# Weight matmuls of a load kept together on TensorE in the input projection's blocks and the values' product

## The chip, the core and the metric

The kernel runs on one core of a Trainium2 chip. The core has a matrix engine (TensorE, PE in the profile, with its weight loads listed as PEld), a vector engine (VectorE, DVE), a scalar engine (ScalarE, ACT), GpSimd (POOL) and SyncE (SP), which here issues the DMAs. Each engine works through its own stream of instructions in order, and semaphores hold an instruction until what it needs is done. The metric is the device time of one execution in microseconds (us). Lower is better.

## What is computed

The reference is a decoder trunk of two layers on one sequence of 256 tokens with 2048 channels. Each layer has a token mixer with two head groups (RWKV-7 time mixing, and sparse attention with three branches) that read one common input projection, then an output projection, a normalization, a squared-ReLU MLP and a second normalization. A conditioning vector gives shifts, scales and gates. Cut to its frame:

```python
for i in range(DEPTH):
    mod = cond @ w_ada[i] + b_ada[i]
    sh_m, sc_m, gt_m, sh_f, sc_f, gt_f = [m[:, None, :] for m in jnp.split(mod, 6, axis=-1)]
    h = x * (1 + sc_m) + sh_m
    u = h @ w_in[i]
    o_rwkv, v_first = _rwkv7_mix(u[..., :RWKV_COLS], v_first, ...)
    o_nsa = _nsa_mix(u[..., RWKV_COLS:], cmp_pos, cmp_w1, cmp_w2)
    y = jnp.concatenate([o_rwkv, o_nsa], axis=-1) @ w_out[i]
    x = _layer_norm(DN_ALPHA * x + (1 + gt_m) * y, ln1_g[i], ln1_b[i])
    h = x * (1 + sc_f) + sh_f
    y = jnp.square(jax.nn.relu(h @ mlp_w1[i])) @ mlp_w2[i]
    x = _layer_norm(DN_ALPHA * x + (1 + gt_f) * y, ln2_g[i], ln2_b[i])
```

All weights are float32 and each is read from memory once.

## The kernel before

**Channels on partitions.** An activation is 16 tiles of 128 channels by 256 tokens. A float32 product is made of three matmuls of a faster 32-bit form: weight and activation are each split into a rounded high part and the rest, and high by high, rest by high and high by rest are added up (`mm3`, L235). The modulated input of a layer is kept as 16 such pairs in the list `hs`: `hhi` and `hlo` in the profile.

**A load.** `unit` (L218) fetches 512 KB of weights into `wf` (5 buffers) by one DMA and splits them in two halves of 512 columns. For each half ScalarE casts `wh` (L226) and VectorE subtracts to get `wl` (L227). `wh` and `wl` have four buffers each, so two loads' worth. `part` gives the slices of 128 (or more) columns.

**A block.** `block` (L243) makes 128 output channels from 16 products: two loads `u` of eight products `k` each, so 2 x 24 weight matmuls of 128x128 by 128x256 into one accumulator bank of PSUM. Two banks exist for it (`acc`). Then `evict` takes the result out; `fill` lets a conditioning step come between loads in layer 0. `block` is called for the input projection `win` with `hs`, for the output projection `wout` with the pairs of `mix`, and for the MLP's `w1` and `w2`. Other forms of the same products are `kouter` (several outputs side by side) and `start` (the first columns of layer 0, under an order written by hand); the change leaves them alone.

**The values' product.** The columns of two of the value projections are computed the other way round, tokens on partitions (L814 to L824): eight loads `q`, each with two channel tiles `k`, two token halves `i` and three matmuls of 128x128 by 128x512, into two accumulators `va`, which share the banks of `acc`.

**What stands beside them.** A layer's mixer has, in the order of the text: the r and k columns and `rwkv_a` for four head pairs of the first half (`half_in`); `rwkv_b`, a triangular inverse, mostly on VectorE; `rwkv_c`, a recurrence over four chunks, in which products of 64 columns (`up`, `zp`, `sp`, `op`) alternate with copies on ScalarE and VectorE; `rwkv_out`; four blocks and four more for the compressed, selected and window keys, with `rope` on their results; `compress`; the second half of the recurrence; the values' product; and for each of eight pairs of heads a query block with `rope` and `attend`, a chain of scores (`cs`, `sc`), softmax, transposes (`ct`, `pt`) and outputs (`ot`). In layer 0 groups of eight conditioning products (`gv`, L206, from `ada_pe`) come in between. All these products are small float32 matmuls, mostly of another stationary operand each.

**What sets the order.** A planner orders each engine's stream: among the instructions that are ready by its own estimate of times it takes the one of highest priority, which is the order of the text unless raised by `high_priority`. So a block's weight matmuls, later in the text, go wherever a small product earlier in the text isn't ready yet, one matmul at a time. `issue_after(x)` puts what follows on x's engine behind x. Together, `with tc.issue_after(first), tc.high_priority(3000000)` make a group that follows its first instruction closely; the scores and outputs in `attend` and the conditioning products are grouped in that way already. The chip then runs the stream as planned, whatever the real durations are.

In the 60 blocks of `win` that run through `block` (24 in layer 0, 36 in layer 1) and in the values' product, every weight matmul stands by itself for the planner.

Of the kernel before, what the change touches and what calls it, by code (L numbers as in the profile page):

```python
# [167 lines left out]
def tile_trunk(tc, ap, outT, dbg=None):  # L168
    nc = tc.nc
    V, A, G, PE, SY = nc.vector, nc.scalar, nc.gpsimd, nc.tensor, nc.sync  # L170
    with ExitStack() as ctx:
# [6 lines left out]
        def st(tag, shape, dt=FT, name=None):  # L178
            if dbg is not None:
                dbg.setdefault("_sz", {})  # L180
                dbg["_sz"][tag] = max(dbg["_sz"].get(tag, 0), int(np.prod(shape[1:])) * 4 * BUFS.get(tag, 1))
            return sb.tile(shape, dt, name=name or tag, tag=tag, bufs=BUFS.get(tag, 1))
# [7 lines left out]
        def accb(shape, name="acc", tag="acc"):  # L190
            return psp.tile(shape, FT, name=name, tag=tag, bufs=2)
# [13 lines left out]
        def mm(o, l, r, start=True, stop=True):  # L205
            return PE.matmul(o, l, r, start=start, stop=stop, skip_group_check=True)  # L206
# [11 lines left out]
        def unit(src):  # L218
            wf = st("wf", [128, 1024])
            SY.dma_start(wf, src)  # L220
            out = []
            for i in range(2):
                wh, wl = st("wh", [128, 512], FR), st("wl", [128, 512], FR)
                s = slice(i * 512, i * 512 + 512)
                with tc.high_priority(1000000):
                    A.copy(wh, wf[:, s])  # L226
                    V.tensor_sub(wl, wf[:, s], wh.bitcast(FT))  # L227
                out.append((wh, wl))

            def part(o, n=128):  # L230
                s = slice(o % 512, o % 512 + n)
                return out[o // 512][0][:, s], out[o // 512][1][:, s]
            return part

        def mm3(o, w, x, first, last):  # L235
            (wh, wl), (xh, xl) = w, x
            mm(o, wh, xh, first, False)
            mm(o, wl, xh, False, False)
            mm(o, wh, xl, False, last)
# [3 lines left out]
        def block(src, u0, xs, evict, rot=False, prio=500000):  # L243
            bank = accb([128, 2, T])
            acc = bank[:, 0]
            for u in range(2):
                w = unit(src[u0 + u])
                for k in range(8):
                    mm3(acc, w(k * 128), xs[u * 8 + k], u + k == 0, u * 8 + k == 15)
                if fill[0]:  # L250
                    fill[0](1)
                count[0] += 1
            with tc.high_priority(prio):
                evict(acc, bank[:, 1]) if rot else evict(acc)
# [103 lines left out]
        hs = []  # L358
# [51 lines left out]
        for l in range(NL):  # L410
# [7 lines left out]
            win = ap["win"][l]  # L418
# [20 lines left out]
            if l == 0:  # L439
                with tc.manual_schedule(engines={PE.engine}):  # L440
                    for _ in first(0):
                        pass
                    sums = [st("TM", [128, 2, T], name="sum") for _ in range(6)]
                    pair = st("SV", [128, 2, 2, T], name="sum")
                    sums += [pair[:, 0], pair[:, 1]] + [st("TM", [128, 2, T], name="sum") for _ in range(2)]
                    start(win, hs, first, sums)
                for b in range(16):
                    ev0(b, sums[b // 2][:, b % 2])
            else:
                kouter(win, 0, hs, ev0)  # L450
                for b in range(8, 12):
                    block(win, 16 + 2 * (b - 8), hs, lambda acc, b=b: ev0(b, acc))
# [227 lines left out]
            def half_in(half):  # L680
                H = {"UR": [[None] * 2 for _ in range(4)], "TM": [[None] * 2 for _ in range(4)], "BK": [[None] * 2 for _ in range(4)],
                     "bv": [None] * 4, "SV": [st("SV", [128, 4, 4, 64], name="SV") for _ in range(2)],
                     "PC": st("PC", [128, 4, 4])}
                for p in range(4):
                    pi = half * 4 + p
                    for i in range(2):
                        b = 12 + 2 * pi + i
                        if l > 0 or b >= NS:
                            block(win, 2 * b if half == 0 else 2 * (b + 8), hs, lambda acc: ev0(b, acc))
                        elif b >= 16:  # L690
                            ev0(b, sums[b // 2][:, b % 2])
                    rwkv_a(pi, p, rkt.pop(2 * pi), rkt.pop(2 * pi + 1), H)
                return H
# [41 lines left out]
            u = 40  # L735
            cin = [[None] * 2 for _ in range(2)]
            for kv in range(2):
                for gp in range(2):
                    t = slab(name="cin")
                    cin[kv][gp] = t  # L740
                    block(win, u, hs, lambda acc, rp, t=t: rope(acc, rp, t) if kv == 0 else A.copy(t, acc), True)
                    u += 2
# [70 lines left out]
            u = 72  # L813
            va = [accb([128, 512], "va") for _ in range(2)]  # L814
            for q in range(8):
                w = unit(win[u + q])
                for k in range(2):
                    xh, xl = hs[2 * q + k]
                    wh, wl = w(k * 512, 512)
                    for i in range(2):  # L820
                        c = slice(i * 128, i * 128 + 128)
                        mm(va[i], xh[:, c], wh, q + k == 0, False)
                        mm(va[i], xl[:, c], wh, False, False)
                        mm(va[i], xh[:, c], wl, False, q + k == 8)  # L824
            u += 8
            Vt = []
            for i in range(2):
# [77 lines left out]
            for j in range(8):  # L905
                q = st("rk" if j < 4 else "S", [128, T], name="q")
# [165 lines left out]
            hs = []  # L1072
# [11 lines left out]
            y = [st("TM", [128, 2, T], name="y") for _ in range(8)]  # L1084
# [43 lines left out]
            if l == 0:  # L1128
                hs = []
# [25 lines left out]
```

## Time and profile before

| what | value |
|---|---|
| median of the runs | 2805.02 us (3 runs, 2801.45 to 2806.73) |
| the profiled execution | 2805.57 us, span of its core 2803.7 us |
| granted TensorE clock, mean | 0.981 |
| weight casts on ScalarE and subtractions on VectorE | 1536 each |
| input projection by `block`, layer 0 | 24 blocks, 48 loads, 1152 weight matmuls |
| input projection by `block`, layer 1 | 36 blocks, 72 loads, 1728 weight matmuls |
| values' product, per layer | 8 loads, 96 weight matmuls |

The profile comes from one execution. Its page has the busy time of each engine, the chain of work that ended last, and the costliest groups of instructions; a line such as L206 is the line of a helper (`mm`), so the tile names tell which product is meant. The timeline lists instructions by start time and merges equal neighbours. Ends of matmuls are modelled and overlap, so the distance from one start to the next is the better measure of pace. The busy time by stretch has a row for each stretch, with each engine's busy time, the granted clock and the DMA share.

### The profile page before, as it was taken

To read this page: it belongs to the slowest core of one execution; us is meant where nothing else is said; L and a number is where in the kernel's file an instruction comes from. 1 tells how busy PE (TensorE), PEld (TensorE's weight loads), DVE (VectorE), ACT (ScalarE), POOL (GpSimd) and SP (SyncE) were. 2 spreads that over 40 slices of the span, in tenths; PEclk is the share of its full clock that TensorE was granted. 3 is DMA by queue.
4 is the path that set the end of the run, shared out by engine and by line. 5 is a ranking of instruction groups with operands and counts; after the bars stand their busy time and mean duration, and the time that the engine had idled before them with its cause. 6 is when DMAs were issued, how large, how long until landed. Compare 5 with 4: busy or idle time off the path is not lost.

```text
span 2803.7 us, 59395 instructions
## 1 busy us (share of the span) xinstructions
PE 2682.2 (96%) x22794; PEld 2450.1 (87%) x22794; DVE 2088.5 (74%) x4710; ACT 1507.1 (54%) x3221; POOL 69.6 (2%) x205
## 2 busy tenths in 40 slices
PE   6999899998999999999999999999999999999997
PEld 4777678756999999999999888887799999999997
DVE  3677868656789788888998786886796566666567
ACT  3344345554585554645557544556567565464555
POOL 0000010000000000000000001000000000000000
PEclk9999999898999999999999999999999999999998
DMA  8986656386579899999986444333466777776664
GB/s 302 320 271 229 239 190 196 121 265 211 171 231 370 316 344 339 338 352 336 342 266 200 140 150 129 120 107 119 157 197 187 235 217 235 231 233 205 195 191 126
DMA packets 206780, 639.63 MB, mean 228 GB/s; under 512 B 23392, under 2 KB 42848, under 8 KB 206496
## 3 DMA queue, kind: packets, MB, share of 16 engines
q1 hardware_dynamic: 206496, 635.83, 68.0%
q8 instruction: 179, 2.93, 0.4%
q14 instruction: 105, 0.86, 0.1%
HBM read 629.45 MB, written 6.29 MB: 227 GB/s over the span
## 4 chain that ended last, share of the span: by engine, by line
PE 78%; DVE 13%; DMA 4%; ACT 3%; issue 2%; SPq 0%; ACTq 0%; POOL 0%; DVEq 0%
PE acc L206 65%; DVE wl L227 4%; PE gv L206 2%; DMA wap<-in_wad 1%; ACT wh L226 1%; PE ot L206 1%; PE pt L896 1%; PE mt L206 1%; DMA wf<-in_win 1%; DVE Tt L577 1%; DVE fs L575 1%; PE va L206 1%; PE vp L206 1%; PE tp L206 0%; PE rb L206 0%
## 5 line engine op out<-in xcount | busy, mean ns | idle before, releaser
L226 ACT CAST wh<-wf 128x512 fp32r<-128x512 f32 x1536 | 946.1, 620 | 859.0 <-PE acc L206 483.4
L227 DVE TENSOR_TENSOR wl<-wf,wh 128x512 fp32r<-128x512 f32 x1536 | 1038.5, 689 | 384.2 <-ACT wh L226 372.8
L206 PE MATMUL acc<-hhi,wh 128*128 128x256 f32 x3456 | 983.5, 285 | 17.1 <-ACT wh L226 8.8
L206 PE MATMUL acc<-hhi,wl 128*128 128x256 f32 x3456 | 972.3, 281 | 8.7 <-DVE wl L227 8.5
L206 PE MATMUL acc<-hlo,wh 128*128 128x256 f32 x3456 | 971.9, 282 | 0.2 <-DVE hlo L407 0.2
L206 PE MATMUL acc<-hi,wh 128*128 128x256 f32 x2560 | 714.8, 279 | 8.1 <-DVE res L1059 3.8
L206 PE MATMUL acc<-lo,wh 128*128 128x256 f32 x2560 | 715.4, 280 | 1.3 <-DVE lo L215 1.3
L206 PE MATMUL acc<-hi,wl 128*128 128x256 f32 x2560 | 714.8, 279 | 0.1
L206 PEld LDWEIGHTS acc<-hhi,wh 128*128 128x128 f32 x3456 | 656.8, 190 | 61.2 <-issue 24.1
L206 PEld LDWEIGHTS acc<-hhi,wl 128*128 128x128 f32 x3456 | 655.7, 190 | 18.2 <-DVE wl L227 12.9
L206 PEld LDWEIGHTS acc<-hlo,wh 128*128 128x128 f32 x3456 | 654.6, 190 | 8.7 <-issue 4.5
L206 PEld LDWEIGHTS acc<-hi,wh 128*128 128x128 f32 x2560 | 484.6, 189 | 10.5 <-ACT hi L214 5.0
L206 PEld LDWEIGHTS acc<-lo,wh 128*128 128x128 f32 x2560 | 483.3, 189 | 3.6 <-DVE lo L215 2.4
L206 PEld LDWEIGHTS acc<-hi,wl 128*128 128x128 f32 x2560 | 484.1, 189 | 1.4 <-issue 0.8
L344 DVE CUSTOM_DVE_ANT_0 wa<-wa,cond,modh 128x1024 f32<-128x1024 f32 x112 | 143.3, 1279 | 0.0
L344 DVE CUSTOM_DVE_ANT_0 wa<-wa,cond,vec 128x1024 f32<-128x1024 f32 x112 | 143.3, 1279 | 0.0
L206 PE MATMUL gv<-wap,cT 128*32 128x512 f32 x640 | 90.6, 639 | 21.7 <-DMA wap<-in_wad 21.4
L1099 DVE TENSOR_TENSOR lo<-relu,hi 128x256 fp32r<-128x256 f32 x128 | 54.1, 425 | 45.5 <-ACT relu L1098 45.3
L288 DVE TENSOR_TENSOR sum<-sum,acc 128x512 f32<-128x512 f32 x70 | 48.1, 687 | 45.8 <-PE acc L206 45.8
L883 ACT ACTIVATE P<-P,tyn 128x128 f32<-128x128 f32 (+1 forms) x128 | 57.3, 448 | 11.8 <-DVE tyn L881 11.1
L1097 ACT ACTIVATE hi<-relu 128x256 fp32r<-128x256 f32 x128 | 53.5, 422 | 3.5
L1098 ACT ACTIVATE relu<-relu 128x256 f32<-128x256 f32 x128 | 53.3, 420 | 3.6
(290 smaller groups left out, 2352.5 us busy)
## 6 DMA issues: line engine op xcount, KB each, us to landing
wf<-in_w SPq DMA_DIRECT2D x512, 512.0 KB, 4.6
wa<-in_wada SPq DMA_DIRECT2D x224, 512.0 KB, 5.6
wf<-in_win SPq DMA_DIRECT2D x192, 512.0 KB, 4.1
wap<-in_wad SPq DMA_DIRECT2D x208, 256.0 KB, 4.7
wf<-in_wout SPq DMA_DIRECT2D x64, 512.0 KB, 4.1
wap<-in_wad SPq DMA_DIRECT2D x56, 512.0 KB, 5.1
cw<-in_cw SPq DMA_DIRECT2D x16, 512.0 KB, 4.1
xin<-in_xT SPq DMA_DIRECT2D x16, 128.0 KB, 5.5
```

The costliest lines, as they stand in the source:

```text
L206: return PE.matmul(o, l, r, start=start, stop=stop, skip_group_check=True)
L226: A.copy(wh, wf[:, s])
L227: V.tensor_sub(wl, wf[:, s], wh.bitcast(FT))
L288: V.tensor_add(s, s, bank)
L344: V.tensor_tensor_reduce(wa, wa, cb, 0.5, init, OP.mult, OP.add, dst)
L575: V.tensor_mul(x, Mu[:, j + 1:32, j:j + 1].to_broadcast([128, n, w]), Tt[:, j:j + 1, 0:w].to_broadcast([128, n, w]))
L577: V.tensor_sub(Tt[:, j + 1:32, 0:w], Tt[:, j + 1:32, 0:w], x)
L883: A.activation(P[:, h, c:c + n], P[:, h, c:c + n], AF.Exp, bias=m[:, 2 * h + i:2 * h + i + 1], scale=-1.0, accum_out=z[:, 2 * h + i:2 * h ...
L896: PE.transpose(pt[:, h, c * 128:c * 128 + 128], P[:, h, 256 * i + c * 128:256 * i + c * 128 + 128], ident)
L1097: A.activation(hi, t, AF.Square)
L1098: A.activation(t, t, AF.Square)
L1099: gate[0] = V.tensor_sub(lo, t, hi.bitcast(FT)).ins
```

## The change

In `block`, when the source is the input projection and the activations are `hs`, the 24 weight matmuls of a load are issued in another order and as a group. The products go from `k` = 7 down to 0, and in each from `wl` by `hhi` over `wh` by `hhi` to `wh` by `hlo`, so that the first matmul reads the second half's `wl`, which is the last operand to be made. The other 23 follow it directly at raised priority. The accumulator's start flag moves to the new first matmul of the first load and the stop flag to the last of the second. All other calls of `block` keep the old order.

In the values' product the 12 matmuls of a load are grouped in the same way: channel tile 1 before 0, the products with `wl` first, both token halves in turn.

```diff
--- before.py
+++ after.py
@@ -245,8 +245,16 @@
             acc = bank[:, 0]
             for u in range(2):
                 w = unit(src[u0 + u])
-                for k in range(8):
-                    mm3(acc, w(k * 128), xs[u * 8 + k], u + k == 0, u * 8 + k == 15)
+                if xs is not hs or src is not win:
+                    for k in range(8):
+                        mm3(acc, w(k * 128), xs[u * 8 + k], u + k == 0, u * 8 + k == 15)
+                else:
+
+                    trio = lambda k: [(w(k * 128)[i], xs[u * 8 + k][j]) for i, j in ((1, 0), (0, 0), (0, 1))]
+                    ops = [o for k in range(7, -1, -1) for o in trio(k)]
+                    with tc.issue_after(mm(acc, *ops[0], u == 0, False).ins), tc.high_priority(3000000):
+                        for i, o in enumerate(ops[1:]):
+                            mm(acc, *o, False, u == 1 and i == 22)
                 if fill[0]:
                     fill[0](1)
                 count[0] += 1
@@ -814,14 +822,16 @@
             va = [accb([128, 512], "va") for _ in range(2)]
             for q in range(8):
                 w = unit(win[u + q])
-                for k in range(2):
+                ops = []
+                for k in range(1, -1, -1):
                     xh, xl = hs[2 * q + k]
                     wh, wl = w(k * 512, 512)
-                    for i in range(2):
-                        c = slice(i * 128, i * 128 + 128)
-                        mm(va[i], xh[:, c], wh, q + k == 0, False)
-                        mm(va[i], xl[:, c], wh, False, False)
-                        mm(va[i], xh[:, c], wl, False, q + k == 8)
+                    for x, y in ((xh, wl), (xh, wh), (xl, wh)):
+                        ops += [(i, x[:, i * 128:i * 128 + 128], y) for i in range(2)]
+                run = lambda n: mm(va[ops[n][0]], *ops[n][1:], q == 0 and n < 2, q == 7 and n >= 10)
+                with tc.issue_after(run(0).ins), tc.high_priority(3000000):
+                    for n in range(1, 12):
+                        run(n)
             u += 8
             Vt = []
             for i in range(2):
```

## The prediction

> **What bounds the kernel now.** First the page: how long the span is, which engine is full, what the chain that ended last is made of.
>
> ```profile
> span 2803.7 us, 59395 instructions
> ...
> PE 2682.2 (96%) x22794; PEld 2450.1 (87%) x22794; DVE 2088.5 (74%) x4710; ACT 1507.1 (54%) x3221; POOL 69.6 (2%) x205
> ...
> PE 78%; DVE 13%; DMA 4%; ACT 3%; issue 2%; SPq 0%; ACTq 0%; POOL 0%; DVEq 0%
> ```
>
> TensorE bounds the kernel on average. The change touches only the stretches that hold the projection's blocks, so the next view is the busy time by stretch: two of layer 0, two of layer 1, and one of the MLP to compare with.
>
> ```profile
> core 0: us, PE busy (x) PEld busy (x) DVE busy (x) ACT busy (x) POOL busy (x), PEclk, DMA share, GB/s
> 2200.00:2300.00 100.00, 100.00 (x879) 100.00 (x878) 56.67 (x87) 55.50 (x105) 0.00 (x0) 1.00 0.67 208
> ...
> 200.00:475.00 275.00, 259.51 (x2109) 202.93 (x2108) 209.21 (x583) 127.99 (x322) 23.43 (x75) 0.95 0.65 218
> 475.00:665.00 190.00, 174.94 (x1510) 120.65 (x1510) 114.36 (x452) 103.92 (x316) 5.62 (x12) 0.92 0.56 186
> 1520.00:1830.00 310.00, 297.85 (x2445) 260.13 (x2445) 243.60 (x637) 158.67 (x371) 20.53 (x71) 0.99 0.44 136
> 1830.00:2006.00 176.00, 164.01 (x1527) 130.54 (x1525) 125.31 (x463) 108.72 (x321) 5.56 (x10) 0.98 0.34 108
> ```
>
> In the MLP 879 matmuls start in 100 us: one per 0.114 us, the pace of a weight matmul in an unbroken row. The four stretches are 951 us long and hold 897 us of busy TensorE. They are nearly full too, but there the weight matmuls are mixed with the small float32 products of the recurrence and of the attention. The timeline of TensorE shows what the mixing costs (start, duration, instruction):
>
> ```profile
> 1723.05 0.69 PE L206 MATMUL zp<-Us,TM 128*64 128x64 f32 x16
> 1723.66 0.38 PE L206 MATMUL acc<-hlo,wh 128*128 128x256 f32 x1
> 1723.89 0.28 PE L206 MATMUL acc<-hhi,wh 128*128 128x256 f32 x1
> 1724.00 0.29 PE L206 MATMUL acc<-hhi,wl 128*128 128x256 f32 x1
> 1724.12 0.28 PE L206 MATMUL acc<-hlo,wh 128*128 128x256 f32 x1
> 1724.38 0.30 PE L206 MATMUL sp<-ZV,BK 128*64 128x64 f32 x2
> 1724.61 0.39 PE L206 MATMUL acc<-hhi,wh 128*128 128x256 f32 x1
> ```
>
> Four weight matmuls stand between two small products. From the first's start to the next small product's start is 1724.38 - 1723.66 = 0.72 us, where four at the unbroken pace are 0.46. The second starts 0.23 after the first instead of 0.11, and the small product 0.26 after the last instead of 0.11. I call such a stretch of weight matmuls a **run**. Over all runs of the four stretches I took the time from a run's first start to the next other start, less 0.114 per matmul: the median is 0.21 us, whatever the run's length. That is the price of going in and out of a run once.
>
> Then I counted. The projection's block matmuls stand in 131 runs in layer 0 (first and last start below) and 131 in layer 1.
>
> ```profile
> 204.36 0.47 PE L206 MATMUL acc<-hhi,wh 128*128 128x256 f32 x1
> ...
> 599.26 0.39 PE L206 MATMUL acc<-hhi,wh 128*128 128x256 f32 x1
> ...
> 1522.30 0.47 PE L206 MATMUL acc<-hhi,wh 128*128 128x256 f32 x1
> ...
> 1925.48 0.37 PE L206 MATMUL acc<-hlo,wh 128*128 128x256 f32 x1
> ```
>
> The 24 blocks of layer 0 and 36 of layer 1 are 120 loads of 24 matmuls. Numbering the matmuls shows 222 breaks inside a load, in 78 of the 120 loads, and 40 between loads; 176 of the runs are seven matmuls or shorter.
>
> **The change, part by part.** No matmul, cast or load is added or taken away, and no DMA is moved past a queue. Two things change: the order of TensorE's stream, and the moment from which a load may start.
>
> Switches removed. After the change a load's 24 matmuls are one run, so there are at most 120 runs where 262 were: 142 fewer at 0.21 us, **-30 us**. This is the careful end: where loads follow each other without a break, as many do already, there are fewer runs still. If all 222 inner breaks went and none came between loads, it would be 222 x 0.21 = 47 us.
>
> The small products' side. A group of them that is torn by a run costs more as well:
>
> ```profile
> 1727.98 0.30 PE L206 MATMUL up<-SV,UR 128*64 128x64 f32 x2 [0.42 <-DVE SV L640]
> 1728.21 0.39 PE L206 MATMUL acc<-hlo,wh 128*128 128x256 f32 x1
> ...
> 1728.65 0.68 PE L206 MATMUL up<-SV,UR 128*64 128x64 f32 x14
> 1729.26 0.39 PE L206 MATMUL acc<-hhi,wl 128*128 128x256 f32 x1
> ```
>
> Here 16 products take 0.23 + 0.61 = 0.84 us in two pieces; the 16 of zp above take 0.61 in one. Most groups are not torn but wait for another engine between them, so I take nothing and keep 142 x 0.23 = 33 us as the far end.
>
> At this switch a rule of the Trainium skill speaks against the change. TensorE: Matmul & The Clock Gate, "Part 2: What happens when you issue a matmul", says that TensorE pulls weight loads ahead of matmuls in flight, so that the next tile's weights load while the last one's matmul runs. By it a switch would cost nothing and the 30 us above would be zero. The weight loads of the same run disagree:
>
> ```profile
> 1723.66 0.19 PEld L206 LDWEIGHTS acc<-hlo,wh 128*128 128x128 f32 x1
> 1723.77 0.19 PEld L206 LDWEIGHTS acc<-hhi,wh 128*128 128x128 f32 x1
> ```
>
> The second load starts 0.12 before its matmul (1723.89); the first starts with its matmul, not before it. In this trace the pull-ahead stops at the switch.
>
> The values' product. Its 16 loads of 12 matmuls stand in 21 runs now, of which the first six-matmul run is this:
>
> ```profile
> 441.78 0.59 PE L206 MATMUL va<-wh,hhi 128*128 128x512 f32 x1
> ...
> 443.36 0.50 PE L206 MATMUL tp<-cst,a 128*128 128x2 f32 x4
> ```
>
> Six take 1.58 us, 0.20 more than six at its usual 0.23. At least five runs go: **-1 us**.
>
> Pauses that lose their cover. The short runs are what the planner slips in while a small product waits for VectorE or ScalarE. One such stretch, the recurrence over four chunks of the first half in layer 1, by groups, and its busy time:
>
> ```profile
> L206 PE MATMUL acc<-hlo,wh 128*128 128x256 f32 x20 | 6.3, 317 | 0.0
> L206 PE MATMUL acc<-hhi,wh 128*128 128x256 f32 x20 | 6.1, 306 | 0.0
> L206 PE MATMUL acc<-hhi,wl 128*128 128x256 f32 x20 | 6.0, 301 | 0.0
> ...
> L206 PE MATMUL up<-SV,UR 128*64 128x64 f32 x48 | 2.9, 229 | 1.1 <-DVE SV L640 0.9
> ...
> 1711.00:1735.00 24.00, 22.94 (x347) 19.33 (x347) 11.16 (x21) 9.40 (x34) 8.32 (x18) 1.00 0.19 59
> ```
>
> 60 weight matmuls in 16 runs fill the pauses so well that TensorE is idle for one of 24 us. The recurrence runs four times (two halves, two layers), with 13, 16, 12 and 13 runs and 190 weight matmuls: 190 x 0.114 / 54 = 0.40 us a pause. 190 matmuls are eight loads. A load of 24 x 0.114 = 2.7 us covers one pause and overruns it, so 46 pauses would stand open: 46 x 0.40 = 18 us. If the other half's products, the attention's or more loads stand ready, it is nothing. I take the middle, **+10 us**.
>
> What is late next is the attention, eight heads one after the other up to 665 and 2006. Where nothing covers its pauses they look like this:
>
> ```profile
> 649.94 0.93 PE L206 MATMUL sc<-Kd,q 64*128 64x128 f32 x8 [1.01 <-DVE tyn L881]
> ...
> 652.35 1.21 PE L206 MATMUL ot<-cts,vcb 32*128 32x256 f32 x2 [1.16 <-DVE tyn L881]
> ...
> 655.28 1.12 PE L206 MATMUL ot<-pts,Vt 128*64 128x256 f32 x4 [0.67 <-ACT pts L898]
> ```
>
> The added wait. A load now starts when its last operand, the second wl, is there, and not at the first wh; behind its first matmul TensorE's in-order stream is held, small products included. Who waits for casts today, and what a cast costs:
>
> ```profile
> L226 ACT CAST wh<-wf 128x512 fp32r<-128x512 f32 x1536 | 946.1, 620 | 859.0 <-PE acc L206 483.4
> L227 DVE TENSOR_TENSOR wl<-wf,wh 128x512 fp32r<-128x512 f32 x1536 | 1038.5, 689 | 384.2 <-ACT wh L226 372.8
> ...
> PE acc L206 <- ACT wh L226: 5.1, 4, 2.6
> ```
>
> Between 200 and 480 TensorE waited four times for a wh. A second cast pair behind it is 0.62 + 0.69 = 1.31 us, so 4 x 1.31 = **+5 us**. Elsewhere casts wait for TensorE (483 us of ScalarE's idle time), which is the cover. It gets thinner: buffers of two loads exist, and the first-half operands are now read last, so the cast of the load after next waits until a load is nearly through. The last pair is then ready 1.31 us after the end of a load while the next one runs 2.7 us: 1.4 us of slack. If VectorE eats that in all 120 loads by 0.2 us, it is 24 us; I take none.
>
> The sum: -30 - 1 + 10 + 5 = **-16 us**. The profiled execution took 2805.57 us, of which the span is 2803.7; the median of the runs shown is 2805.02, so it is an ordinary one. 2805.6 - 16 = **2789.6 us**.
>
> **The rivals.** (1) Slower: the pauses stay open. The same mechanism as the +10, everywhere. 142 runs vanish, each the filling of a pause of about 0.40 us; the saved switch pays 0.21 of it. If all stood open, it would be 142 x 0.40 - 31 + 5 = +31 us. It decides for slower from about 65 open pauses on (65 x 0.40 = 26). For it: in layer 0 the 48 loads are spread over 131 runs, and only two block banks and four r/k buffers let loads run ahead. Against: TensorE has other small work in most of these places, 28 groups of conditioning products among it. With 95 open it is 38 - 31 + 5 = +12: 2818 us. (2) A draw: about 60 stand open, 24 - 31 + 5 = -2: 2804 us. (3) The clock. The stretches were granted 0.95, 0.92, 0.99 and 0.98 of it: 275 x 0.05 + 190 x 0.08 + 310 x 0.01 + 176 x 0.02 = 36 us at most. If dense runs bring all of that back, the time is 2789.6 - 36 = 2754 us. The same page, under "Loop structure matters more than you think", says that matmuls kept back to back keep the clock up; the windows above have 1.00 in the MLP and 0.92 in the stretch with the fewest weight matmuls, so the trace doesn't exclude it. (4) The change doesn't do what it says: the planner orders by its own estimate, other work of the same raised priority stands between the matmuls of a load, and 262 runs remain: 2806 us.
>
> **How the numbers follow.** A measurement can tell about 0.2% (5.6 us) from no change: faster is under 2799.4, slower over 2810.6. The forecast: 0.52. Rival 1: 0.21. Rival 2: 0.15. Rival 3: 0.07. Rival 4: 0.05. Faster 0.52 + 0.07 = 0.59, same 0.15 + 0.05 = 0.20, slower 0.21. The range: low end by the clock's or the small products' far end (2754, or 2789.6 - 33 = 2757), taken at 2756; high end 2821, rival 1 with 102 open pauses (41 - 31 + 5 = +15). The forecast's own range is 2770 to 2799.
>
> **What would show it.** In the timeline of the changed kernel every load's 24 matmuls start 0.11 us apart, with wl first and no break; the runs are at most 120. The stretches at 200 to 665 and 1520 to 2006 together get shorter by some 16 us, and the MLP stays. In the recurrence TensorE's idle time before up, zp and op grows from one in 24 us; if it grows by over 6 us in each of the four, rival 1 has it. Waits of acc for wl replace those for wh. The prediction is wrong in its mechanism if the runs fall to 120 and busy TensorE time in the stretches does not fall by about 30 us.

## The result, and the profile after

| | before | changed |
|---|---|---|
| median | 2804.79 us | 2838.59 us |
| ratio | 1 | 1.0121 (95% interval 1.0098 to 1.0145) |
| profiled execution, span of its core | 2803.7 us | 2840.4 us |

The change makes the kernel slower by 1.2%. The forecast was 2789.6 us with a range up to 2821: wrong in sign, and outside the range.

First the page of the changed kernel, the lines that answer to those of before:

```profile
span 2840.4 us, 59258 instructions
...
PE 2679.0 (94%) x22794; PEld 2455.2 (86%) x22794; DVE 2088.8 (74%) x4710; ACT 1508.1 (53%) x3221; POOL 69.6 (2%) x205
```

No engine has more to do. TensorE's busy time is even 3 us less while the span is 37 us longer, so its gaps grew by 40 us. (Busy time is no measure of work alone: a small product counts for longer at half clock.) The busy time by stretch says where. The mixer of a layer (from about the end of its modulated input to the start of the MLP's) before, layers 0 and 1:

```profile
187.00:766.00 579.00, 540.13 (x4440) 426.01 (x4440) 406.89 (x1205) 286.39 (x744) 30.00 (x93) 0.94 0.62 204
1511.00:2077.00 566.00, 538.32 (x4587) 465.85 (x4586) 437.77 (x1255) 307.05 (x764) 26.19 (x82) 0.98 0.45 143
```

and after (columns as before: PE, PEld, DVE, ACT, POOL, granted clock, DMA share, GB/s):

```profile
187.00:775.00 588.00, 531.20 (x4437) 418.98 (x4438) 409.35 (x1203) 286.79 (x743) 30.39 (x93) 0.93 0.61 201
1522.00:2117.00 595.00, 543.72 (x4593) 477.95 (x4592) 436.36 (x1258) 308.02 (x765) 25.76 (x82) 0.92 0.43 136
```

Layer 0's mixer is 9 us longer and layer 1's 29, which is the loss. TensorE's idle time in the two grew from 66.6 to 108.1 us, and the clock of layer 1 fell from 0.98 to 0.92.

**A ledger of TensorE.** In these two mixers I gave the time from each matmul's start to the next one's to the first of the two, and summed it by kind. "Runs" counts unbroken rows of the projection's matmuls, the values' included; half clock is the time for which the profile grants 0.5.

| kernel | runs | projection and values, us | small products, us | output projection, us | half clock, us |
|---|---|---|---|---|---|
| before | 284 | 492.6 | 438.1 | 214.4 | 92 |
| changed | 107 | 441.4 | 514.7 | 227.1 | 181 |
| difference | -177 | -51.2 | +76.6 | +12.7 | +89 |

The switches were saved, more than forecast: 51.2 / 177 = 0.29 us a run. But from the starts of the same small products 77 us more pass, and the sum is +38 us, the loss in span. By the clock record of the two traces, 71 of these 77 us passed at half clock (46 us before, 117 after). The idle time, 41 us more, lies mostly outside the four recurrences: in them it grew from 3.7 to 7.3 us, and the rest stands in the head pairs (18 us), the inverses (10) and the attention with what follows it (10).

### The profile page after: what moved, and what is told of

Same layout as the page of the kernel before. It is cut to its first block, busy times and chain, and to the rows that moved or that the text cites. A ratio compares the mean times of both kernels' runs of the same rounds, so it can differ in the third digit from the quotient of the medians.

```text
span 2840.4 us, 59258 instructions
## 1 busy us (share of the span) xinstructions
PE 2679.0 (94%) x22794; PEld 2455.2 (86%) x22794; DVE 2088.8 (74%) x4710; ACT 1508.1 (53%) x3221; POOL 69.6 (2%) x205
## 4 chain that ended last, share of the span: by engine, by line
PE 77%; DVE 13%; ACT 4%; DMA 3%; issue 2%; SPq 0%; ACTq 0%; POOL 0%; DVEq 0%
PE acc L206 64%; DVE wl L227 4%; PE gv L206 2%; PE va L206 2%; DMA wf<-in_win 2%; DMA wap<-in_wad 1%; ACT wh L226 1%; PE ot L206 1%; DVE Tt L585 1%; DVE fs L583 1%; PE pt L906 1%; PE sc L206 1%; PE tp L206 0%; PE up L206 0%; PE vp L206 0%
## 5 line engine op out<-in xcount | busy, mean ns | idle before, releaser
L206 PE MATMUL acc<-hhi,wh 128*128 128x256 f32 x3456 | 966.2, 280 | 11.3 <-ACT hhi L413 7.3
L206 PE MATMUL acc<-hlo,wh 128*128 128x256 f32 x3456 | 961.9, 279 | 0.2 <-DVE hlo L415 0.2
L206 PEld LDWEIGHTS acc<-hhi,wl 128*128 128x128 f32 x3456 | 655.2, 190 | 34.7 <-DVE wl L227 25.1
L908 DVE COPY pts<-pt 128x256 f32<-128x256 f32 x32 | 13.5, 423 | 65.2 <-PE pt L906 65.0
```

Source lines behind the costliest of these rows:

```text
L908: last_ins[0] = (A.copy if i == 0 else V.tensor_copy)(pts, pt).ins
```

## The experiments

**Theories.** *Pauses*: whole loads overrun the pauses of the small products' chains, hold the chains up, and are then missing in later pauses. *Wait*: the loss is the late start, on a load's last operand, and the buffers held longer. *Values*: it sits in the values' product. *Clock*: it is the half clock.

The first four runs part the change. Each is compared with the kernel before on the same chip, and its trace is read as in the ledger.

`e1_blocks_only`: the values' product as before.

> The projection's blocks are grouped as in the change, the values' product is left as before. If the loss sits in the block loads (their 24 matmuls overrun a pause of the small products and then are missing in the next pauses), the time is near the changed kernel's: 2833 to 2843 us, with about 90 runs of block matmuls and a lower granted clock in the stretches of the recurrence. If the values' product carries the loss, it is within 5 us of 2805.

`e2_values_only`: the blocks as before.

> Only the values' product is grouped, the blocks are as before. If the loss sits in the block loads: 2800 to 2810 us, since only some five of 21 runs at 0.2 us go. If the values' product carries it: 2825 to 2840.

`e3_order_only`: the changed order of the 24 matmuls, but no group:

```diff
-with tc.issue_after(mm(acc, *ops[0], u == 0, False).ins), tc.high_priority(3000000):
-    for i, o in enumerate(ops[1:]):
-        mm(acc, *o, False, u == 1 and i == 22)
+for i, o in enumerate(ops):
+    mm(acc, *o, u + i == 0, u == 1 and i == 23)
```

> The block matmuls go in the changed order (products 7 to 0, the second half's wl first) but each stands by itself for the planner again; values as before. Theory pauses (grouping costs, the late start does not): 2800 to 2815 us, some 260 runs as before. Theory wait (the cost is that a load starts only with its last operand and holds its four cast buffers longer): 2825 to 2840 us, with longer waits of acc for wl.

`e4_halves`: a group for each half of a load, 12 matmuls, the half's own `wl` first; values as before:

```diff
-ops = [o for k in range(7, -1, -1) for o in trio(k)]
+for h in range(2):
+    ops = [o for k in range(4 * h + 3, 4 * h - 1, -1) for o in trio(k)]
...
```

> Groups of 12: the four products of each half of a load are one group, the half's wl first; values as before. Theory pauses: the overrun of a pause is 1.4 us in place of 2.7, so the loss falls to between a third and a half: 2810 to 2822 us. Theory wait: the first matmul of a group waits for its own half's wl only, so most of the loss goes: 2800 to 2808. If neither size nor order matters but grouping as such: 2833 to 2843.

| run | ratio (95% interval) | median, us | before on its chip | runs | projection | small products |
|---|---|---|---|---|---|---|
| e1_blocks_only | 1.0072 (1.0052 to 1.0093) | 2822.29 | 2803.01 | 125 | 445.6 | 495.4 |
| e2_values_only | 1.0011 (0.9996 to 1.0026) | 2807.81 | 2803.01 | 281 | 491.0 | 443.2 |
| e3_order_only | 1.0009 (0.9993 to 1.0026) | 2802.62 | 2803.01 | 302 | 498.0 | 439.3 |
| e4_halves | 0.9986 (0.9967 to 1.0005) | 2797.29 | 2803.01 | 180 | 455.8 | 459.2 |

The wait falls: with the late start alone no loss can be told. Nor can one for the values alone. The blocks carry most, though less than I expected (2833 to 2843), so the two parts together cost more than apart, if barely beyond the intervals. Why stays open. From the end of the first recurrence to the last `mt` product of the second half's head pairs, layer 0 takes 76 us before, 78 with the blocks grouped and 92 with both, and layer 1 takes 84, 74 and 88; but with both parts each of these stretches holds 120 more block matmuls than with the blocks alone, which are 14 us of work at 0.114 each, so the lengths don't locate a loss. What differs most is the half clock in the mixers: 92 us before, 109 with the blocks grouped, 181 with both. Halves keep 37 us of the saving and lose 21 in the small products; the time ended below all expected ranges, but the interval of the ratio reaches 1.

**Where the chains are held up.** The inverse of the first half in layer 1 shows it; its 31 steps on VectorE begin when the four head pairs are through. By the tile's instructions, with first and last start, before and after:

```profile
L575 DVE TENSOR_TENSOR fs<-Mu,Tt x31: 192/353/424, 1646.4 to 1692.9; 128x31 f32<-128x31 f32 x2, 128x60 f32<-128x60 f32 x2, 128x87 f32<-128x87 f32 x2, 128x112 f32<-128x112 f32 x2
```

```profile
L583 DVE TENSOR_TENSOR fs<-Mu,Tt x31: 191/359/502, 1696.1 to 1739.0; 128x31 f32<-128x31 f32 x2, 128x60 f32<-128x60 f32 x2, 128x87 f32<-128x87 f32 x2, 128x112 f32<-128x112 f32 x2
```

The last cast of the layer's modulated input began at 1510.9 before and 1522.5 after. Counted from there, the inverse begins 135.5 us into the layer before and 173.6 after: 38 us later. By then 284 more of the projection's matmuls have run, so most of the 38 us is work done early, and not time lost at this point. One link of such a chain in TensorE's timeline (start, duration), before:

```profile
1602.16 0.46 PE L552 MATMUL bkt<-cst,a 64*128 64x64 f32 x4
...
1603.10 1.09 PE L206 MATMUL vp<-cst,vt 128*64 128x128 f32 x8
```

and after:

```profile
1600.58 0.46 PE L560 MATMUL bkt<-cst,a 64*128 64x64 f32 x4 [1.11 <-ACT TM L557]
1600.97 0.39 PE L206 MATMUL acc<-hhi,wl 128*128 128x256 f32 x1
...
1603.71 0.28 PE L206 MATMUL acc<-hlo,wh 128*128 128x256 f32 x1
1603.91 1.09 PE L206 MATMUL vp<-cst,vt 128*64 128x128 f32 x8
```

From `bkt` to `vp` it is 0.94 us before, with two block matmuls between, and 3.33 after, with 24. A load once begun can't be broken. And what was spent here is missing later. The recurrence of the same half, after, by one step in the timeline and by busy time (columns as above; before, 62 block matmuls stand between its first `up` and its last `op`):

```profile
1763.67 1.12 PE L206 MATMUL zp<-Us,TM 128*64 128x64 f32 x16 [0.52 <-ACT Us L625]
```

```profile
1755.00:1781.00 26.00, 21.27 (x312) 18.64 (x311) 8.30 (x18) 5.44 (x24) 6.35 (x13) 0.50 0.00 1
```

No block matmul is left in it and TensorE runs at half clock. It is no shorter: from the first `up` to the last `op` 25.1 us before and 25.6 after. The half clock has a part in that. In `e1_blocks_only` the same recurrence stands alone too, but at a mean clock of 0.78; a step of its full-clock part, and its busy time:

```profile
1758.62 0.69 PE L206 MATMUL zp<-Us,TM 128*64 128x64 f32 x16 [0.52 <-ACT Us L625]
```

```profile
1739.20:1761.30 22.10, 16.36 (x306) 14.19 (x304) 7.74 (x17) 5.43 (x24) 5.98 (x12) 0.78 0.01 2
```

From the first `up` to the last `op` it takes 22.0 us there. The pause is the same 0.52 us, but the 16 products take 0.69 us in place of 1.12. Carried on in a straight line from 25.6 us at 0.50 over 22.0 at 0.78, a recurrence alone at full clock would take some 20 us; that is an estimate. By it the 62 block matmuls, 7 us of work at 0.114, and ten other products made the recurrence some 5 us longer before: the pauses hid a part of their time, and not all of it.

The second four runs test size, place and clock.

`e5_quarters`: groups of six. `e6_a0_single`: the changed kernel, but in layer 1 the r and k blocks of the first half and the four of the compressed branch stand singly. `e8_layer0_blocks`: whole loads in layer 0's blocks alone. `e7_cover`: the changed kernel with four dummy matmuls into each accumulator of the recurrence ahead of its products (the first product's start flag clears them, so they leave nothing in the result):

```diff
+def cover(t):
+    for _ in range(4):
+        mm(t.rearrange("p a b -> p (a b)"), hs[0][0][:, 0:128], hs[0][0])
...
 zp = mx("c", [128, 4, 64], "zp")
+cover(zp)
```

> Groups of six block matmuls (two products, 0.7 us), the values as before. Theory pauses: six matmuls last hardly longer than a pause, so the small chains are not held up and the switches of the shortest runs still go: 2785 to 2800 us, at or below the halves (2797). If smaller groups only bring the kernel back to before: 2800 to 2808.

> The changed kernel, but in layer 1 the r and k blocks of the first half and the four blocks for the compressed branch stand by themselves again (24 of 72 loads). The changed kernel's first head pairs of layer 1 were 38 us late by the time their triangular inverse began. Theory pauses, with the loss where loads overtake the chain of the head pairs: that delay goes (under 12 us left of 38) and the time falls to 2800 to 2818. If the loss sits in the recurrence itself or in the clock, the delay at that point does not matter and it stays at 2828 to 2843.

> The changed kernel with four dummy matmuls of 128x256 (0.46 us at full clock) into each accumulator of the recurrence before its products, 60 matmuls per recurrence, so TensorE is busy in its pauses as before the change. Theory clock (the half-speed clock in the uncovered recurrences makes the loss): the clock of the recurrences returns to 1 and the time falls by 12 us or more, to 2815 to 2827. Theory delay (chains held up elsewhere): 2833 to 2850, since dummies do nothing for that.

> Whole-load groups in layer 0's blocks alone; layer 1 and the values as before. In the run with only blocks grouped layer 0 ended 8 us earlier than before and layer 1 took some 28 us longer. If that holds: 2792 to 2800 us. If layer 0's gain was the clock's chance: 2800 to 2815.

| run | ratio (95% interval) | median, us | before on its chip | runs | projection | small products | half clock |
|---|---|---|---|---|---|---|---|
| e5_quarters | 1.0041 (1.0021 to 1.0060) | 2804.60 | 2798.21 | 235 | 481.4 | 459.1 | 140 |
| e6_a0_single | 1.0103 (1.0061 to 1.0144) | 2824.27 | 2798.21 | 136 | 440.7 | 499.0 | 125 |
| e7_cover | 1.0206 (1.0168 to 1.0243) | 2853.69 | 2798.21 | 108 | 448.3 | 536.0 | 143 |
| e8_layer0_blocks | 0.9998 (0.9982 to 1.0014) | 2796.62 | 2798.21 | 203 | 461.7 | 464.1 | 79 |

The small products of `e7` include its dummies. `e6` and `e7` ended outside both of their ranges, `e5` in that of the rival; `e8` lies at the time expected of a gain, but before was as fast on its chip. With `e6` the delay at the inverse went as the theory says; the tile's instructions there:

```profile
L583 DVE TENSOR_TENSOR fs<-Mu,Tt x31: 182/349/424, 1652.1 to 1698.1; 128x31 f32<-128x31 f32 x2, 128x60 f32<-128x60 f32 x2, 128x87 f32<-128x87 f32 x2, 128x112 f32<-128x112 f32 x2
```

The last cast of its modulated input began at 1515.8, so this is 136.3 us in, as before the change. But the time hardly fell. The loads that didn't overtake the chain there met it in the recurrence: 264 whole-load matmuls in place of 62, and 45.6 us in place of 25.1. The 202 more are 23 us of work at 0.114, so this too is work done early; and, as in the changed kernel, no block matmul is left for the second half's recurrence, where 32 stood before. The lack of fill moves to a later place. Quarters should have beaten halves and did not: 49 runs fewer than before saved 11 us and the small products took 21 more. In layer 0 alone whole loads gain 31 us in switches and lose 26 again: a draw.

`e7` kept TensorE busy in the recurrences. Layer 1's first one ran at half clock for 6 us instead of all 26, and still took 25.1 us. The kernel got slower by about the dummies' own time (some 240 x 0.114 = 27 us). That doesn't part the clock from the dummies. So I asked once more, with dummies in the first half alone.

`e13_cover_first`: the changed kernel, as `e7` but in the first half's inverse and recurrence only.

> The changed kernel with dummy matmuls in the first half's inverse and recurrence alone (six before each of hp and xp, four before each of up, zp, sp and op), where no block matmul is left in layer 1 and TensorE ran at half clock for 44 us. Theory clock (the half clock there is a large part of the loss): the half clock of layer 1 falls from some 95 us to under 55 and the time to 1.002 to 1.008 of before. Theory delay (the chains of the head pairs are held up and the recurrence is a chain whose length the clock hardly changes): 1.010 to 1.016, as the changed kernel's 1.0121 or a little above.

It measured 1.0169 (1.0146 to 1.0192), median 2852.42 us beside 2802.08: above both ranges. The same stretch, columns as above:

```profile
1763.00:1788.00 25.00, 24.46 (x354) 20.67 (x353) 6.91 (x15) 5.44 (x24) 5.42 (x11) 0.87 0.01 1
```

The clock there is 0.87 in place of 0.50, the recurrence 25.3 us in place of 25.6, and layer 1's mixer 594.9 in place of 594.8; layer 0's, where loads still fill the recurrence, is 8 us longer with the dummies. Layer 1's half clock fell by 20 us only, not by the 40 expected, so the run doesn't settle the layer. Nor does it clear the clock in the recurrence. Its two middle chunks take 6.7 and 6.8 us at half clock in the changed kernel, 6.1 and 6.2 at full clock with the dummies, and 5.2 and 5.5 at 0.96 and 1.00 alone, in `e10_but_queries` below: the dummies took back over half of what the clock gave. So in the recurrence the half clock costs time, as `e1` shows too.

Three runs ask which blocks: `e9_queries` groups whole loads in the query blocks alone, `e10_but_queries` in all others, `e11_halves_queries` halves in the others and whole loads in the queries; values as before in all.

> Whole-load groups in the query blocks alone (16 of 48 loads in layer 0, 16 of 72 in layer 1), all else as before. Theory delay (whole loads hold up the chains of the head pairs, then are missing in the recurrences; the query loads come behind the last head pairs): 0.993 to 0.999 of before, from some 40 switches less, with the head pairs' times as before. Theory cover (every open pause costs, those of the attention and of the second recurrence too): 1.002 to 1.010.

> The complement: whole-load groups in all projection blocks but the queries. Theory delay: the loss of the run with all blocks grouped (1.0072) is here or more, 1.005 to 1.013, and layer 1's first triangular inverse begins over 30 us later in the layer than before (135.5 us after its start). Theory cover: less than half of it, 0.998 to 1.004.

> Groups of 12 in all blocks but the queries, whole loads in the queries, values as before: the mildest form where chains run beside the blocks. If halves hold the chains up little and whole query loads cost nothing: 0.992 to 0.999. If not additive: 0.999 to 1.004.

| run | ratio (95% interval) | median, us | before on its chip | runs | projection | small products |
|---|---|---|---|---|---|---|
| e9_queries | 1.0026 (1.0012 to 1.0041) | 2807.18 | 2800.65 | 218 | 471.8 | 463.5 |
| e10_but_queries | 1.0086 (1.0060 to 1.0111) | 2824.61 | 2800.65 | 181 | 470.8 | 482.3 |
| e11_halves_queries | 0.9995 (0.9978 to 1.0013) | 2799.98 | 2800.65 | 168 | 452.8 | 469.4 |

`e10` came as expected, with the inverse 174.9 us into the layer. `e9` came as its rival said: the queries come behind the head pairs, but the second recurrence and the attention run beside them, and 21 us of switches cost 25 in small products. In none of the places tried were whole loads a gain. `e11` came out as not additive.

`e14_halves_again`, to narrow the one promising form:

> The groups of 12 once more, to narrow 0.9986 (0.9967 to 1.0005). If halves are the right size: 0.996 to 0.999, clear of 1. If the gain was chance: 0.999 to 1.002.

0.9986 (0.9964 to 1.0008), 2797.18 us beside 2802.08. Twice the same, and twice the interval reaches 1: halves are no slower than before, and a gain of some 0.1% isn't proved. No form tried beats the kernel before beyond what can be told.

## Why the prediction was wrong

- **Switches, -30 us: the mechanism was right, the size too small.** 177 runs went where 147 were forecast as the least, and each gave 0.29 us, not 0.21: -51 us. The price was a median. A sum goes by the mean, and over the same runs of the kernel before the mean is 0.33, since some of them are far longer. (The four stretches hold 896 us of busy TensorE, not 897; nothing hangs on it.) Over the variants the projection's time follows the number of runs roughly (455.8 and 470.8 us at 180 and 181 runs).
- **The rule on weight loads** of the Trainium skill (TensorE: Matmul & The Clock Gate, "Part 2: What happens when you issue a matmul"): the prediction's reading of it, that a switch would be free, doesn't hold here, since removing switches removed time. The page ties the pull-ahead to conditions (row groups that don't conflict, or a load into the background weight buffer); whether they fail at a switch, no run here shows.
- **The values' product, -1 us.** Grouped alone, its 21 runs became 13 and its own time fell from 50.9 to 47.5 us; what it does to the chains beside it was left out.
- **The added wait, +5 us: right.** Between 200 and 490 the waits of acc for wl are 10.9 us after (row below), where acc waited 5.1 + 2.1 = 7.2 for wh and wl before; in the whole execution they grew from 17.3 to 21.4. The order alone measured 1.0009.

```profile
PE acc L206 <- DVE wl L227: 10.9, 8, 4.3
```

- **Pauses that lose their cover, +10 us: the step that failed.** It priced 46 open pauses at 0.40 us in the four recurrences, at an unchanged clock, and took half. In its place the runs showed +77 us in the small products and +13 in the output projection. The recurrences, where it looked, account for 4 of the 41 us by which TensorE's idle time grew. It named the other side ("covers one pause and overruns it") and left it without a price: in the link shown above a load holds the chain by 2.4 us (3.33 against 0.94), and loads so run early, 284 matmuls in one half of one layer, are missing as fill later. And it put the clock of what is left uncovered at nothing. That it is the grouping by whole loads is shown: the same order without a group, and groups of 12, lose nothing that can be told, and whole loads in the blocks 0.7%.
- **Rival 1 had the sign and half of the mechanism.** With every pause open it came to 2837 us, near the 2838.59 measured, but by luck: its own sign, over 6 us more idle time in each of the four recurrences, did not come (0.8, 0.7, 1.1 and 1.1 us before; 0.3, 0.7, 4.7 and 1.6 after). The sign of a wrong mechanism, busy TensorE time that does not fall by some 30 us, did come: in the two mixers it fell by 3.5.
- **The clock, rival 3, went the other way.** The prediction let it only rise. Half clock in the profiled executions grew from 109 to 224 us. The Trainium skill (TensorE: Matmul & The Clock Gate, "Loop structure matters more than you think") shows an idle wait of 8 us between matmuls as what drops the clock. The trace agrees in part: the 44 us at 0.50 around the recurrence that lost its loads begin in a wait of 4.6 us (`hp` for VectorE, 1742.2 to 1746.9). But they last although no pause behind it is longer than 0.67 us, and 10 us at 0.50 from 1962.7 on come with no pause over 0.42 in the 7 us before.
- **How much of the loss is the slower clock stays open, but it isn't little.** Executions of one kernel have one stream, and still differ: halves took 2785.82 us at a mean clock of 0.983 and 2808.59 at 0.972. Counting the missing clock as time at half, that is some 63 us more of it and 23 us more time. Over all 199 executions with a clock on record, each set against the mean of its kernel on its chip, 0.29 us go with each us of half clock (correlation 0.75). The changed kernel has a mean clock of 0.966 against 0.980 before, some 81 us more half clock: by that rate 24 of its 34 us. This is an estimate from what goes together, and not a proof, since longer gaps also bring a lower clock. It isn't all: `e1`, at 0.976, loses 20 us, of which the rate gives 6, while TensorE's idle time in its mixers is 33 us above that of before.

## What to carry to other kernels

A long piece of work that fills another chain's pauses is worth most when it can be cut to the pause. Grouping it saves switches, here 0.2 to 0.35 us each, but a group that is longer than the pause holds up the chain, and the fill then runs out before the chain does. Beside the switches, ask where the fill will be missing later, what the gaps there cost, and what clock the uncovered products will be granted. Where an engine is busy for 94% of a stretch, freeing one chain of the fill, as `e6` did, can move the lack to the next. And price a sum by a mean, not by a median.

## What the runs showed of the hardware

- A recurrence of 64-column float32 products that stood alone on TensorE took 25.6 us at a granted clock of 0.50 and 22.0 at 0.78 (and 22.0 at 0.81 in `e10`). Its pause before `zp` was 0.52 us at either clock, while the 16 products of `zp` took 1.12 us at half clock and 0.69 at full.
- Uncovered small products did not bring the full clock back at once: after a wait of 4.6 us the changed kernel ran 44 us on end at 0.5 around that recurrence, `e1` 17 us after the same wait. Four matmuls of 128x256 before each step (`e7`) left 6 of the recurrence's 25 us at half clock.
- One kernel, with one stream, was granted another mean clock from one execution to the next: `e14` 0.971 in 2804.13 us and 0.984 in 2781.2.
